# A decoder layer on one core: stacks by way of DRAM, output weights in the chunk stream, the last head by token halves, a third pair of heads

## The chip, the core and the metric

The kernel runs on one core of a Trainium2 chip. A core has five engines with instruction streams of their own: TensorE (PE, matmuls; PEld is its weight load), VectorE (DVE), ScalarE (ACT), GpSimd (POOL) and SyncE (SP), which here issues nearly all DMAs; 16 DMA engines move the data. The metric is the device time of one execution in microseconds, lower is better.

## What is computed

One layer of a decoder with two groups of four heads, 1024 tokens, model width 1024, all float32:

```python
u = rmsnorm(h, norm_pre_w)
dq, dk, dv, dg, rq, rk, rv, rg = split(u @ w_in)          # 8 x 512 columns
y_a = diff_attention(dq, dk, dv, positions, lam)          # p0 - lam * p1, causal softmax, rotary
y_a = rmsnorm(y_a, diff_subln_w) * (1 - lambda_init) * silu(dg)
y_b = rmsnorm(retention_chunkwise(rq, rk, rv, positions)) * silu(rg)
y = concat(y_a, y_b) @ w_out
out = h + rmsnorm(y, norm_post_w)
```

A differential head has two components (u = 0, 1) of 64 dimensions; each has its own scores and softmax, and the second probability matrix is subtracted, times lambda, from the first. Retention works in chunks of 128 tokens with a running state.

## The kernel before

Heads are numbered in the order of work, `HEADS = [0, 4, 1, 5, 2, 6, 3, 7]`: even places are differential heads, odd ones retention heads. Below, "head 6" is the head at place 6.

*Precision.* A float32 factor is split in a high and a low part (`whi`/`wlo` for weights, `uh`/`ul` for the input, `yh`/`yl` for the mixed heads), and every product is three matmuls: high x high, high x low, low x high.

*Main order.* `main_steps` walks through `ORDER`: projection blocks "qk" (queries and keys of one head; `cols_steps`, L404 to 421, lines L414 to L416, four groups g of 24 matmuls 512 wide, g // 2 is the half of the tokens, g % 2 the half of the rotation) and "vg" (values and gates; `rows_steps`, L386 to 402, lines L396 to L398, eight token tiles). A vg block of two heads has matmuls 512 wide, one of a single head 256 wide. In short: v01 q0 v23 q1 q2 v4 q3 q4 v5 q5 q6 v6 q7 v7, then the output projection `out_steps` (L766) for eight token tiles. v01 stands apart (`first_rows`, L377).

*Side streams.* `run` (L940) interleaves the main order with four streams: `score_stream` (scores and softmax of differential heads, `diff_scores` L531, two matmuls per component and piece of keys, L543), `value_stream` (transposes L599, values L612), `ret_stream` (L882; `ret_scores` L644 with transposes L650 and products L657, `ret_states` L669, `ret_out` L692/L693) and `last_stream` (L923; `prep_tile` L745 multiplies a tile of y by its gates, L749, transposes it, L758, and splits it). A step runs when a planner's clock has reached what it waits for; a main step is 1.36 us of matmuls. This order is worked out while the kernel is built and is then fixed: PE and SP run their instructions in exactly this order, so an instruction whose data is late holds up all behind it. The other engines' order is chosen by the scheduler.

*SP's queue.* All DMAs go through `dma` (L124): the planner books 0.6 us each. Moves and stores that are to be issued later wait in a list with a due time (`late`, L129), and `flush` (L134) issues those that are due as long as the booked queue is at most 1.0 us ahead of the clock.

*Weights.* `pump` (L225) fetches chunks of weights (128 x 512, 256 KB) four ahead into `raw`, and splits them (ACT copy L212, subtraction L190) into nine slots `whi`/`wlo`, which `drop_chunk` frees. A chunk is due 4.0 us after its fetch and 3.0 us after its split.

*Stacks.* A differential head's scores contract, in one matmul, the high and low parts: rows of the stack `ks` (128 partitions = hi 64, lo 64) and `qs` (128 partitions = the same 64 rows twice). `diff_qk` (L502) rotates a half of the tokens (`rotate`, L482, lines L490 to L499), splits it into `rhi` and `rlo` (L511, L190; one buffer each), and `move` (L514) copies it with 24 DMAs of 32 partitions (64 KB) from SBUF to SBUF: for each component u, part x and rotation half r one into `ks` and two into `qs`. They are due 4.0 us after the rotation's matmuls. When the last one of a component is issued, `ready` is set to its queue time + 3.6 us, and `score_stream` waits for it.

*Output weights.* `fetch_wout`, `split_wout` and `load_wout` (L709 to L734) read 16 tiles of `w_out` through the same `raw` buffers and split them on ACT (L727) and DVE (L728): columns 512 to 1023 (nh = 1) in places `block_steps` and `main_steps` name around v7, columns 0 to 511 (nh = 0) during v7, into the memory of `uh0`/`ul0`, which is read up to token tile 3 of the last block.

Of the kernel before, what the change touches and what calls it, by code (L numbers as in the profile page):

```python
# [10 lines left out]
F32 = mybir.dt.float32  # L11
F32R = mybir.dt.float32r
# [8 lines left out]
P = 128  # L21
# [4 lines left out]
H = 4  # L26
# [12 lines left out]

HEADS = [0, 4, 1, 5, 2, 6, 3, 7]
ORDER = [("vg", 0, 1), ("qk", 0), ("vg", 2, 3), ("qk", 1), ("qk", 2), ("vg", 4), ("qk", 3), ("qk", 4),
         ("vg", 5), ("qk", 5), ("qk", 6), ("vg", 6), ("qk", 7), ("vg", 7)]

CHUNKS = [(b, c) for b, blk in enumerate(ORDER) for c in range(8 if len(blk) == 3 else 4)]


def shape_constants():
# [38 lines left out]
def body(ctx, tc, x, xt_in, pos, wpk, wout, vecs, npre, npost, subln, cst, out):  # L88
# [101 lines left out]
        eng.tensor_tensor(dst, full, hi.bitcast(F32), op=ALU.subtract)  # L190

    raws, chunks, due_in, due_out = {}, {}, {}, {}
    ahead = {"fetched": 0, "split": 0, "held": 0}

    def fetch_chunk(pieces=1):

        b, c = CHUNKS[ahead["fetched"]]
        raw = raws[b, c] = wraw.tile([P, 512], F32, tag="raw", name="raw")
        for k in range(pieces):
            ks = slice(512 // pieces * k, 512 // pieces * (k + 1))  # L200
            dma(raw[:, ks], wpk[ahead["fetched"], :, ks])
        due_in[b, c] = queue[0] + 4.0
        ahead["fetched"] += 1

    def split_chunk(pieces=1):
        b, c = CHUNKS[ahead["split"]]
        raw = raws.pop((b, c))
        hi = whi.tile([P, 512], F32R, tag="whi", name="whi")
        lo = wlo.tile([P, 512], F32R, tag="wlo", name="wlo")
        for k in range(pieces):  # L210
            ks = slice(512 // pieces * k, 512 // pieces * (k + 1))
            nc.scalar.copy(hi[:, ks], raw[:, ks])  # L212
            split_lo(lo[:, ks], raw[:, ks], hi[:, ks])
        chunks[b, c] = (hi, lo)
        due_out[b, c] = clock[0] + 3.0
        ahead["split"] += 1
        ahead["held"] += 1

    def drop_chunk(b, c):

# [4 lines left out]
    def pump():  # L225

        while True:
            f, n = ahead["fetched"], ahead["split"]
            if f < len(CHUNKS) and (f < 4 or due_out.get(CHUNKS[f - 4], 1e9) <= clock[0]):
                fetch_chunk()  # L230
            elif n < f and ahead["held"] < NWB and due_in[CHUNKS[n]] <= clock[0]:
                split_chunk()
            else:
                return

    def ready(b, c):
        return lambda: due_out.get((b, c), 1e9) <= clock[0]

    def weight(b, kt):

# [261 lines left out]
    def diff_qk(st, g, ps):  # L502
        rotated = rotate(st, g, ps, (cosD, sinD))
        if rotated is None:
            return
        sl, o1, o2 = rotated
        need("m", 0)
        hi = dp["rot"].tile([P, 2, HT], F32R, tag="rhi", name="rhi")
        lo = dp["rot"].tile([P, 2, HT], F32R, tag="rlo", name="rlo")
        for r, o in enumerate((o1, o2)):  # L510
            nc.scalar.copy(hi[:, r, :], o)  # L511
            split_lo(lo[:, r, :], o, hi[:, r, :])

        def move(u, x, r):  # L514
            if (g, u, x, r) == (1, 0, 0, 0):

                st["q"] = dp["stk"].tile([P, 2, 2, S], F32R, tag="qs", name="qs")
                st["k"] = dp["stk"].tile([P, 2, S], F32R, tag="ks", name="ks")
            q0, k0, src = u * 32, 64 + u * 32, (hi, lo)[x]
            d = 64 * x + 32 * r  # L520
            mv(st["k"][d:d + 32, u, sl], src[k0:k0 + 32, r, :])
            for twice in range(2):
                d = 64 * twice + 32 * r
                mv(st["q"][d:d + 32, u, x, sl], src[q0:q0 + 32, r, :])
            if x and r:
                st["ready", g // 2, u] = queue[0] + 3.6

        for k in range(8):
            late(4.0, lambda k=k: move(k // 4, k // 2 % 2, k % 2), "m")

    def diff_scores(st, i, u):  # L531

# [171 lines left out]


    fp = {}
    wo = {"s": const.tile([P, 1], F32, name="wos")}

    def fetch_wout(nh, ms):  # L709
        for m in ms:  # L710
            raw = wraw.tile([P, 512], F32, tag="raw", name="raw")
            dma(raw, wout[HEADS[m] * P:(HEADS[m] + 1) * P, nh * 512:(nh + 1) * 512])
            wo[nh, m] = raw

    def split_wout(nh, ms):

        for m in ms:
            if nh == 0:
                if m == 0:
                    wo["h0"] = upool.tile([P, 8, 512], F32R, tag="uh0", name="woh0")  # L720
                    wo["l0"] = upool.tile([P, 8, 512], F32R, tag="ul0", name="wol0")
                wh, wl = wo["h0"][:, m, :], wo["l0"][:, m, :]
            else:
                wh = whi.tile([P, 512], F32R, tag="whi", name="woh")
                wl = wlo.tile([P, 512], F32R, tag="wlo", name="wol")
            raw, sc = wo[nh, m], wo["s"] if HEADS[m] < H else 0.5
            nc.scalar.activation(wh, raw, AF.Copy, scale=sc)  # L727
            nc.vector.scalar_tensor_tensor(wl, raw, sc, wh.bitcast(F32), op0=ALU.mult, op1=ALU.subtract)  # L728
            wo[nh, m] = (wh, wl)

    def load_wout(nh, ms):
        for m in ms:
            fetch_wout(nh, [m])
            split_wout(nh, [m])  # L734

    def load_y(t):
        yrows[t] = fp["y"].tile([P, D], F32, tag="yt", name="yt")
# [28 lines left out]
    def out_steps(t):  # L766
        rows = slice(t * P, (t + 1) * P)
        yh, yl = fp.pop(t)
        xt = fp["fp"].tile([P, D], F32, tag="xt2", name="xt2")
        dma(xt, x[rows, :])  # L770
        ob = fp["fp"].tile([P, D], F32, tag="ob", name="ob")
        sq = fp["fp"].tile([P, 512], BF16, tag="osq", name="osq")
        ms = sm_.tile([P, 2], F32, tag="ms2", name="ms2")
        for nh in range(2):
            op = bank("op")
            for m in range(8):
                wh, wl = wo[nh, m]
                nc.tensor.matmul(op, lhsT=yh[:, m, :], rhs=wh, start=(m == 0), stop=False)  # L778
                nc.tensor.matmul(op, lhsT=yh[:, m, :], rhs=wl, start=False, stop=False)  # L779
                nc.tensor.matmul(op, lhsT=yl[:, m, :], rhs=wh, start=False, stop=(m == 7))  # L780
                if m in (1, 3, 5):
                    yield 1.36
            sl = slice(nh * 512, (nh + 1) * 512)
            nc.scalar.activation(sq, op, AF.Square, scale=1.0 / math.sqrt(D), accum_out=ms[:, nh:nh + 1])
            if nh == 0:
                nc.vector.tensor_scalar(ms[:, 0:1], ms[:, 0:1], EPS, None, op0=ALU.add)
            else:
                tot = sm_.tile([P, 1], F32, tag="tot", name="tot")
                rsqrt(tot, ms[:, 1:2], ms[:, 0:1])
# [10 lines left out]

    heads = [{"n": n, "h": hh} for n, hh in enumerate(HEADS)]
    done = set()
    def block_steps(b):
        kind, sts = ORDER[b][0], [heads[n] for n in ORDER[b][1:]]
        n, st = ORDER[b][1], sts[0]
        if kind == "vg":
            for m in ORDER[b][1:]:

                yield lambda: m < 4 or ("A", m - 4) in done or ("R", m - 4) in done
            if len(sts) == 2:  # L810
                for t in range(NT):
                    ps = bank("pj")
                    yield from rows_steps(b, t, ps, 0, 1)
                    values_gates(sts, t, ps)
            else:
                for t in range(0, NT, 2):
                    ps = bank("pj")
                    for j in range(2):
                        yield from rows_steps(b, t + j, ps, j, 2)
                    values_gates(sts, t, ps)  # L820
                    if b == NB - 1 and t == 0:
                        fetch_wout(0, range(0, 4))
                    elif b == NB - 1 and t == 2:
                        split_wout(0, range(0, 4))
                        load_wout(0, range(4, 8))
                        fetch_wout(1, range(4, 8))
            return
        for g in range(4):
            if n > 1 and g == 1:

                yield lambda: ("S", n - 2) in done or ("R", n - 2) in done
            ps = yield from cols_steps(b, g)
            (diff_qk if st["h"] < H else ret_qk)(st, g, ps)
            if b == NB - 2 and g == 2:
                fetch_wout(1, range(0, 4))

    def main_steps():
        for b in range(1, NB):
            if b == NB - 1:
                split_wout(1, range(0, 4))  # L840
            yield from block_steps(b)
        split_wout(1, range(4, 8))
        for t in range(NT):
            yield lambda: fp.get(("ready", t), 1e9) <= clock[0]
            yield from out_steps(t)
# [257 lines left out]
```

## Time and profile before

| | us |
|---|---|
| median of three runs | 589.57 |
| lowest and highest run | 587.15, 591.94 |
| the profiled execution | 587.86 |
| its span, first to last instruction | 586.1 |
| PE busy in the span | 569.3 |

The profile belongs to one execution, whose span leaves 1.8 us around it. Matmuls overlap their neighbours, so the mean duration of one is longer than the distance between the starts of two; the distances are what the span is made of.

### The profile page before, as it was taken

Reading aid. Unit: us, or ns where it says so; the run is one execution under the profiler, and the core shown is the slowest. Engines: PE = TensorE matmul, PEld = TensorE weight load, DVE = VectorE, ACT = ScalarE, POOL = GpSimd, SP = SyncE. Lnnn points to the kernel's source line nnn. Section 1 sums busy time; section 2 is a strip of 40 time slices with the busy share of each in tenths; the row PEclk is TensorE's granted clock in tenths of the full one; section 3 lists DMA queues with packets and bytes.
Section 4 is the critical chain, followed back from the end, with each engine's and each line's share of the span. In section 5 each row is a group of like instructions: output and inputs, shape, how many; then the busy total and the mean of one; then the engine's idle time right before and its main releaser. Section 6 shows DMA issues by size and latency. Waiting matters only on the chain.

```text
span 586.1 us, 9508 instructions
## 1 busy us (share of the span) xinstructions
PE 569.3 (97%) x3280; PEld 499.7 (85%) x3280; DVE 321.7 (55%) x798; ACT 244.4 (42%) x682; POOL 133.7 (23%) x182
## 2 busy tenths in 40 slices
PE   6999999999999999999999999999999989999995
PEld 5888878788888999888899888899989978888884
DVE  4794426466355467744655755446775265544432
ACT  6696125457022366451346442336543362212120
POOL 4154221114124302233503032431222000000000
PEclk9999999999999999999999999999999989999999
DMA  8964764305242554112554124164123772455322
GB/s 276 340 242 122 182 163 130 87 20 156 61 107 50 134 129 140 46 55 77 140 132 117 49 47 125 47 158 96 54 54 93 245 242 101 168 181 195 108 73 107
DMA packets 49344, 73.98 MB, mean 126 GB/s; under 512 B 7824, under 2 KB 21520, under 8 KB 49296
## 3 DMA queue, kind: packets, MB, share of 16 engines
q1 hardware_dynamic: 49152, 73.36, 42.9%
q8 instruction: 26, 0.43, 0.3%
q14 instruction: 22, 0.18, 0.1%
q10 hardware_dynamic: 144, 0.00, 0.0%
HBM read 42.41 MB, written 12.06 MB: 93 GB/s over the span
## 4 chain that ended last, share of the span: by engine, by line
PE 93%; DMA 2%; SPq 1%; DVE 1%; issue 1%; ACT 1%; POOL 0%; DVEq 0%; POOLq 0%; ACTq 0%
PE pj L414 10%; PE pj L415 10%; PE pj L416 10%; PE pj L377 8%; PE pj L396 7%; PE pj L397 7%; PE pj L398 7%; PE sc L543 6%; PE o L612 5%; PE op L778 5%; PE op L780 5%; PE op L779 5%; PE tp L599 3%; SPq L127 1%; PE yt L758 1%; PE o L693 1%
## 5 line engine op out<-in xcount | busy, mean ns | idle before, releaser
L180 POOL TENSOR_TENSOR tot<-tot,halves 128x1 f32<-128x1 f32 (+1 forms) x56 | 33.4, 596 | 315.3 <-DVE tot L179 306.4
L414 PE MATMUL pj<-uh,whi 128*128 128x512 f32 x256 | 104.0, 406 | 0.0
L416 PE MATMUL pj<-uh,wlo 128*128 128x512 f32 x256 | 100.1, 391 | 0.0
L415 PE MATMUL pj<-ul,whi 128*128 128x512 f32 x256 | 99.9, 390 | 0.0
L396 PE MATMUL pj<-whi,uh 128*128 128x256 f32 (+1 forms) x320 | 99.5, 311 | 0.0
L398 PE MATMUL pj<-whi,ul 128*128 128x256 f32 (+1 forms) x320 | 97.4, 305 | 0.0
L397 PE MATMUL pj<-wlo,uh 128*128 128x256 f32 (+1 forms) x320 | 97.3, 304 | 0.0
L398 PEld LDWEIGHTS pj<-whi,ul 128*128 128x128 f32 x320 | 60.9, 190 | 2.6
L397 PEld LDWEIGHTS pj<-wlo,uh 128*128 128x128 f32 x320 | 61.0, 191 | 2.4
L396 PEld LDWEIGHTS pj<-whi,uh 128*128 128x128 f32 x320 | 60.9, 190 | 2.4
L416 PEld LDWEIGHTS pj<-uh,wlo 128*128 128x128 f32 x256 | 48.0, 188 | 10.5
L212 ACT CAST whi<-raw 128x512 fp32r<-128x512 f32 (+1 forms) x65 | 39.5, 619 | 41.5 <-PE pj L415 27.9
L414 PEld LDWEIGHTS pj<-uh,whi 128*128 128x128 f32 x256 | 48.2, 188 | 8.5
L415 PEld LDWEIGHTS pj<-ul,whi 128*128 128x128 f32 x256 | 48.3, 189 | 8.4
L778 PE MATMUL op<-woh,yh 128*128 128x512 f32 x128 | 51.4, 401 | 0.3 <-ACT yh L760 0.3
L780 PE MATMUL op<-woh,yl 128*128 128x512 f32 x128 | 50.2, 392 | 0.0
L779 PE MATMUL op<-wol,yh 128*128 128x512 f32 x128 | 50.1, 391 | 0.0
L190 POOL TENSOR_TENSOR wlo<-raw,whi 128x512 fp32r<-128x512 f32 x32 | 41.6, 1307 | 35.8 <-ACT whi L212 35.4
L543 PE MATMUL sc<-ks,qs 128*128 128x384 f32 (+5 forms) x192 | 42.9, 349 | 2.9 <-ACT v L452 1.3
L499 POOL TENSOR_TENSOR o<-o,m 128x512 f32<-128x512 f32 x16 | 27.1, 1694 | 58.9 <-DVE o L496 49.5
L612 PEld LDWEIGHTS o<-v,at 128*128 128x128 f32 x288 | 37.5, 191 | 2.4
L612 PE MATMUL o<-v,at 128*128 128x128 f32 x288 | 38.4, 274 | 0.0
(139 smaller groups left out, 976.5 us busy)
## 6 DMA issues: line engine op xcount, KB each, us to landing
raw<-in_wpk SPq DMA_DIRECT2D x63, 256.0 KB, 3.0
xr<-in_x SPq DMA_DIRECT2D x8, 512.0 KB, 8.7
gdram<-g SPq DMA_DIRECT2D x32, 128.0 KB, 2.1
qs<-rhi SPq DMA_DIRECT2D x64, 64.0 KB, 2.0
qs<-rlo SPq DMA_DIRECT2D x64, 64.0 KB, 2.0
raw<-in_wout SPq DMA_DIRECT2D x16, 256.0 KB, 4.4
gy<-gdram SPq DMA_DIRECT2D x8, 512.0 KB, 4.8
xt<-in_x SPq DMA_DIRECT2D x8, 512.0 KB, 4.0
```

The source lines that it names most:

```text
L377: nc.tensor.matmul(ps, rhs=wp, lhsT=up[half][:, kt, j * P:(j + 1) * P], start=(kt == 0 and n == 0), stop=(kt == KT - 1 and n == 2))
L396: nc.tensor.matmul(dst, lhsT=a, rhs=wh, start=(kt == 0 and j == 0), stop=False)
L397: nc.tensor.matmul(dst, lhsT=a, rhs=wl, start=False, stop=False)
L398: nc.tensor.matmul(dst, lhsT=l, rhs=wh, start=False, stop=(kt == KT - 1 and j == n - 1))
L414: nc.tensor.matmul(ps, lhsT=wh, rhs=uh[half][:, kt, :], start=(kt == 0), stop=False)
L415: nc.tensor.matmul(ps, lhsT=wh, rhs=ul[half][:, kt, :], start=False, stop=False)
L416: nc.tensor.matmul(ps, lhsT=wl, rhs=uh[half][:, kt, :], start=False, stop=(kt == KT - 1))
L543: nc.tensor.matmul(sp[:, 0:kn], lhsT=st["q"][:, u, x, i * P:(i + 1) * P], rhs=st["k"][:, u, k0:k0 + kn], start=(x == 0), stop=(x == 1))
L612: nc.tensor.matmul(o_ps[:, 0:P], lhsT=at[:, j * P:(j + 1) * P], rhs=v[:, j0 + j, :], start=(j0 + j == 0), stop=(j0 + j == i))
L778: nc.tensor.matmul(op, lhsT=yh[:, m, :], rhs=wh, start=(m == 0), stop=False)
L779: nc.tensor.matmul(op, lhsT=yh[:, m, :], rhs=wl, start=False, stop=False)
L780: nc.tensor.matmul(op, lhsT=yl[:, m, :], rhs=wh, start=False, stop=(m == 7))
```

## The change

*Stacks.* `move` gives way to `store` and `load`. For each half of the tokens, four stores of 256 KB (part x, rotation half r; all 128 partitions of `rhi` or `rlo`) go into a DRAM tile `sd`, due 3.0 (x = 0) and 3.7 us (x = 1) after the matmuls; six loads of 256 KB, due at 7.0 us, fill the stacks: per component one for `ks` (hi and lo) and two for `qs` (a broadcast of two copies each). `ready` is set as before, at queue time + 3.6 us. SP waits for the stores before it issues the loads that read them.

*Output weights.* The 16 tiles are appended to the chunks (`STREAM`); `pump` fetches and splits them like chunks, nh = 0 once `ahead["u0"]` is set (after v7a), nh = 1 into free `whi`/`wlo` slots. `out_steps` waits, for tile 0, for each chunk by the planner's clock.

*Halves.* Blocks v6, q7 and v7 are cut into token halves a and b: v01 q0 v23 q1 q2 v45 q3 q4 q5 v6a q6 v6b q7a v7a q7b v7b.

*Third pair.* v4 and v5 become v45, 512 wide, between q2 and q3.

```diff
-ORDER = [("vg", 0, 1), ("qk", 0), ("vg", 2, 3), ("qk", 1), ("qk", 2), ("vg", 4), ("qk", 3), ("qk", 4),
-         ("vg", 5), ("qk", 5), ("qk", 6), ("vg", 6), ("qk", 7), ("vg", 7)]
+PLAN = "v01 q0 v23 q1 q2 v45 q3 q4 q5 v6a q6 v6b q7a v7a q7b v7b".split()
+BLOCKS = list(dict.fromkeys(w.rstrip("ab") for w in PLAN))
+ORDER = [("vg" if w[0] == "v" else "qk",) + tuple(int(c) for c in w[1:]) for w in BLOCKS]
...
+STREAM = CHUNKS + [("out", nh, m) for nh in range(2) for m in range(8)]
...
+            if key[0] == "out":
+                _, nh, m = key
+                dma(raw, wout[HEADS[m] * P:(HEADS[m] + 1) * P, nh * 512:(nh + 1) * 512])
...
+    def room(key):
+
+        return ahead["u0"] if key[:2] == ("out", 0) else ahead["held"] < NWB
...
+        if key[0] == "out":
+
+            sc = wo["s"] if HEADS[key[2]] < H else 0.5
+            nc.scalar.activation(hi, raw, AF.Copy, scale=sc)
+            nc.vector.scalar_tensor_tensor(lo, raw, sc, hi.bitcast(F32), op0=ALU.mult, op1=ALU.subtract)
...
-            if f < len(CHUNKS) and (f < 4 or due_out.get(CHUNKS[f - 4], 1e9) <= clock[0]):
+            if f < len(STREAM) and (f < 4 or due_out.get(STREAM[f - 4], 1e9) <= clock[0]):
                 fetch_chunk()
-            elif n < f and ahead["held"] < NWB and due_in[CHUNKS[n]] <= clock[0]:
+            elif n < f and room(STREAM[n]) and due_in[STREAM[n]] <= clock[0]:
                 split_chunk()
...
-        def move(u, x, r):
-            if (g, u, x, r) == (1, 0, 0, 0):
-
+        sd = dram.tile([2, 4, 2, 32, HT], F32, tag="sd", bufs=2, name="sd")
+
+        def store(x, r):
+            dma(sd[x, :, r], (hi, lo)[x][:, r, :].bitcast(F32))
+
+        def load(u, part):
+            if (g, u, part) == (1, 0, 0):
                 st["q"] = dp["stk"].tile([P, 2, 2, S], F32R, tag="qs", name="qs")
                 st["k"] = dp["stk"].tile([P, 2, S], F32R, tag="ks", name="ks")
-            q0, k0, src = u * 32, 64 + u * 32, (hi, lo)[x]
-            d = 64 * x + 32 * r
-            mv(st["k"][d:d + 32, u, sl], src[k0:k0 + 32, r, :])
-            for twice in range(2):
-                d = 64 * twice + 32 * r
-                mv(st["q"][d:d + 32, u, x, sl], src[q0:q0 + 32, r, :])
-            if x and r:
+            if part == 0:
+                dma(st["k"][:, u, sl].bitcast(F32), sd[:, 2 + u].rearrange("x r p c -> x (r p) c"))
+                return
+            x = part - 1
+            src = sd[x, u].rearrange("r p c -> (r p) c").unsqueeze(0).broadcast_to([2, 64, HT])
+            dma(st["q"][:, u, x, sl].bitcast(F32), src)
+            if x:
                 st["ready", g // 2, u] = queue[0] + 3.6
 
-        for k in range(8):
-            late(4.0, lambda k=k: move(k // 4, k // 2 % 2, k % 2), "m")
+        for x in range(2):
+            for r in range(2):
+                late(3.0 + 0.7 * x, lambda x=x, r=r: store(x, r), "m")
+        for u in range(2):
+            for part in range(3):
+                late(7.0, lambda u=u, part=part: load(u, part), "m")
...
+                if t == 0:
+                    yield ready("out", nh, m)
+                wh, wl = chunks["out", nh, m]
...
+        tokens = (0, NT) if half is None else (half * NT // 2, (half + 1) * NT // 2)
...
-        for g in range(4):
+        for g in range(tokens[0] // 2, tokens[1] // 2):
...
+        last = max(k for k, w in enumerate(PLAN) if w[-1] == "a")
+        for k, w in enumerate(PLAN[1:], 1):
+            yield from block_steps(BLOCKS.index(w.rstrip("ab")), "ab".index(w[-1]) if w[-1] in "ab" else None)
+            ahead["u0"] = k >= last
```

## Rows read from the trace of the kernel before

**Rows 1.** The page's part 1: busy us, share of the span and instructions of each engine.
```profile
PE 569.3 (97%) x3280; PEld 499.7 (85%) x3280; DVE 321.7 (55%) x798; ACT 244.4 (42%) x682; POOL 133.7 (23%) x182
```

**Rows 2.** Waits of PE: line, releaser, us in total, times, longest.
```profile
PE pj L377 <- ACT whi L212: 5.1, 1, 5.1
PE yt L758 <- DVE yt L749: 2.2, 1, 2.2
PE sc L543 <- ACT v L452: 1.3, 1, 1.3
PE sc L543 <- DMA qs<-rlo: 1.1, 1, 1.1
PE sc L543 <- issue: 0.5, 1, 0.5
PE op L778 <- ACT yh L760: 0.3, 1, 0.3
```

**Rows 3.** Timeline of head 7's start and the final projection: start, us, engine, line, operation.
```profile
460.33 0.38 PE L650 MATMUL tp<-ident,kT 128*128 128x128 f32 x2
...
475.06 0.60 PE L758 MATMUL yt<-ident,yt 128*128 128x128 f32 x4
...
476.41 0.74 DVE L728 SCALAR_TENSOR_TENSOR wol<-raw,wos,woh 128x512 fp32r<-128x512 f32 x1
...
477.06 0.68 DVE L749 TENSOR_TENSOR yt<-yt,gy 128x512 f32<-128x512 f32 x1
...
477.89 0.73 PE L758 MATMUL yt<-ident,yt 128*128 128x128 f32 x4 [2.23 <-DVE yt L749]
```

**Rows 4.** Busy us by engine, granted clock, DMA share, GB/s of 475 to 482 us.
```profile
475.00:482.00 7.00, 4.42 (x21) 3.43 (x21) 6.09 (x11) 4.94 (x12) 0.77 (x2) 0.76 0.82 258
```

**Rows 5.** PE's timeline: first and next instruction of two undisturbed stretches, and q2's end.
```profile
263.01 0.39 PE L414 MATMUL pj<-uh,whi 128*128 128x512 f32 x1
...
275.26 0.38 PE L650 MATMUL tp<-ident,kT 128*128 128x128 f32 x2
...
463.72 0.28 PE L397 MATMUL pj<-wlo,uh 128*128 128x256 f32 x1
...
467.91 0.27 PE L693 MATMUL o<-v,sT 128*128 128x128 f32 x1
...
188.82 0.39 PE L693 MATMUL o<-v,sT 128*128 128x128 f32 x2
...
194.50 0.28 PE L396 MATMUL pj<-whi,uh 128*128 128x256 f32 x1
```

**Rows 6.** Timelines of DVE, POOL, SP and PE: head 6's first stacks and its scores.
```profile
371.90 0.69 DVE L495 TENSOR_TENSOR m<-pj,sinD 128x512 f32<-128x512 f32 x1 [0.72 <-PE pj L416]
...
374.46 0.55 SPq L127 DMA_DIRECT2D ks<-rhi  x1
...
376.97 1.29 POOL L190 TENSOR_TENSOR rlo<-o,rhi 128x512 fp32r<-128x512 f32 x1
...
381.02 1.22 SPq L127 DMA_DIRECT2D qs<-rlo  x2
...
386.82 0.34 PE L543 MATMUL sc<-ks,qs 128*128 128x128 f32 x2
...
394.96 1.56 PE L543 MATMUL sc<-ks,qs 128*128 128x128 f32 x10
```

**Rows 7.** DMA issues: tensors, queue, count, KB each, median us from issue to landing.
```profile
raw<-in_wpk SPq DMA_DIRECT2D x63, 256.0 KB, 3.0
...
gdram<-g SPq DMA_DIRECT2D x32, 128.0 KB, 2.1
...
xk<-in_xt SPq DMA_DIRECT2D x8, 256.0 KB, 4.6
```

**Rows 8.** As rows 4, of the first 30 us and of 560 to 580 us.
```profile
0.00:30.00 30.00, 24.86 (x98) 20.35 (x99) 19.23 (x31) 19.76 (x31) 7.58 (x16) 1.00 0.92 310
...
560.00:580.00 20.00, 19.93 (x88) 16.15 (x87) 5.18 (x11) 2.07 (x6) 0.55 (x1) 1.00 0.29 106
```

More of the change, by code (lines that the diff above doesn't have):

```diff
@@ L192, in body @@
     raws, chunks, due_in, due_out = {}, {}, {}, {}
-    ahead = {"fetched": 0, "split": 0, "held": 0}
+    wo = {"s": const.tile([P, 1], F32, name="wos")}
+    ahead = {"fetched": 0, "split": 0, "held": 0, "u0": False}
     def fetch_chunk(pieces=1):
-        b, c = CHUNKS[ahead["fetched"]]
-        raw = raws[b, c] = wraw.tile([P, 512], F32, tag="raw", name="raw")
+        key = STREAM[ahead["fetched"]]
+        raw = raws[key] = wraw.tile([P, 512], F32, tag="raw", name="raw")
         for k in range(pieces):
             ks = slice(512 // pieces * k, 512 // pieces * (k + 1))
-            dma(raw[:, ks], wpk[ahead["fetched"], :, ks])
-        due_in[b, c] = queue[0] + 4.0
+            if key[0] == "out":
+                _, nh, m = key
+                dma(raw, wout[HEADS[m] * P:(HEADS[m] + 1) * P, nh * 512:(nh + 1) * 512])
+            else:
+                dma(raw[:, ks], wpk[ahead["fetched"], :, ks])
+        due_in[key] = queue[0] + 4.0
         ahead["fetched"] += 1
+    def room(key):
+        return ahead["u0"] if key[:2] == ("out", 0) else ahead["held"] < NWB
     def split_chunk(pieces=1):
[L206 to L210, printed above, removed]
+        key = STREAM[ahead["split"]]
+        raw = raws.pop(key)
+        if key[:2] == ("out", 0):
+            if key[2] == 0:
+                wo["h0"] = upool.tile([P, 8, 512], F32R, tag="uh0", name="woh0")
+                wo["l0"] = upool.tile([P, 8, 512], F32R, tag="ul0", name="wol0")
+            hi, lo = wo["h0"][:, key[2], :], wo["l0"][:, key[2], :]
+        else:
+            hi = whi.tile([P, 512], F32R, tag="whi", name="whi")
+            lo = wlo.tile([P, 512], F32R, tag="wlo", name="wlo")
+            ahead["held"] += 1
+        if key[0] == "out":
+            sc = wo["s"] if HEADS[key[2]] < H else 0.5
+            nc.scalar.activation(hi, raw, AF.Copy, scale=sc)
+            nc.vector.scalar_tensor_tensor(lo, raw, sc, hi.bitcast(F32), op0=ALU.mult, op1=ALU.subtract)
+        for k in range(0 if key[0] == "out" else pieces):
             ks = slice(512 // pieces * k, 512 // pieces * (k + 1))
@@ L213, in split_chunk @@
             split_lo(lo[:, ks], raw[:, ks], hi[:, ks])
-        chunks[b, c] = (hi, lo)
-        due_out[b, c] = clock[0] + 3.0
+        chunks[key] = (hi, lo)
+        due_out[key] = clock[0] + 3.0
         ahead["split"] += 1
-        ahead["held"] += 1
     def drop_chunk(b, c):
@@ L234, in pump, with ready @@
                 return
-    def ready(b, c):
-        return lambda: due_out.get((b, c), 1e9) <= clock[0]
+    def ready(*key):
+        return lambda: due_out.get(key, 1e9) <= clock[0]
     def weight(b, kt):
@@ L706, in body @@
     fp = {}
[L707 to L734, printed above, removed]
     def load_y(t):
@@ L776, in out_steps @@
             for m in range(8):
-                wh, wl = wo[nh, m]
+                if t == 0:
+                    yield ready("out", nh, m)
+                wh, wl = chunks["out", nh, m]
                 nc.tensor.matmul(op, lhsT=yh[:, m, :], rhs=wh, start=(m == 0), stop=False)
@@ L802, in body, with block_steps @@
     done = set()
-    def block_steps(b):
+    def block_steps(b, half=None):
         kind, sts = ORDER[b][0], [heads[n] for n in ORDER[b][1:]]
         n, st = ORDER[b][1], sts[0]
+        tokens = (0, NT) if half is None else (half * NT // 2, (half + 1) * NT // 2)
         if kind == "vg":
@@ L810, in block_steps @@
             if len(sts) == 2:
-                for t in range(NT):
+                for t in range(*tokens):
                     ps = bank("pj")
@@ L815, in block_steps @@
             else:
-                for t in range(0, NT, 2):
+                for t in range(*tokens, 2):
                     ps = bank("pj")
@@ L820, in block_steps @@
                     values_gates(sts, t, ps)
[L821 to L826, printed above, removed]
             return
-        for g in range(4):
+        for g in range(tokens[0] // 2, tokens[1] // 2):
             if n > 1 and g == 1:
@@ L833, in block_steps @@
             (diff_qk if st["h"] < H else ret_qk)(st, g, ps)
-            if b == NB - 2 and g == 2:
-                fetch_wout(1, range(0, 4))
     def main_steps():
[L838 to L842, printed above, removed]
+        last = max(k for k, w in enumerate(PLAN) if w[-1] == "a")
+        for k, w in enumerate(PLAN[1:], 1):
+            yield from block_steps(BLOCKS.index(w.rstrip("ab")), "ab".index(w[-1]) if w[-1] in "ab" else None)
+            ahead["u0"] = k >= last
         for t in range(NT):
```

## The prediction

> **What bounds the kernel now.** I read the page's busy times first, then the waits of TensorE (PE), then its timeline. PE is busy for 569.3 of 586.1 us, VectorE for 55%, ScalarE and GpSimd for less, and the weight loads run beside the matmuls [rows 1]: time goes only if PE gets less work or waits less. All its waits are six, 10.5 us together [rows 2]; the first (5.1 us, first weights) is not touched. Two places are within the change's reach. Early, the first head's scores wait 1.1 us for a stack, 0.5 us more without a shown cause (I read it as the other component's stack) and 1.3 us for a drained bank. Late, at 475 us, the final projection is late. There the second half of the first y tile is transposed 2.23 us late, because VectorE had splits of output weights (L728, the last one 0.74 us at 476.41) ahead of the product (L749) [rows 3]. From 475 to 482 us the granted clock is 0.76 [rows 4], that is, 24% of 7 us = 1.7 us lost at the lower of its two levels. With the waits of 2.2 and 0.3 us [rows 2] this place costs 4.2 us. After PE's last matmul comes a tail of some 6 us, unchanged.
>
> **The change, part by part.**
>
> *Third pair 512 wide.* Matmuls of 512 columns start 54 in 12.25 us, 0.2269 us each; those of 256 columns 35 in 4.19 us, 0.1197 us each [rows 5]. Blocks v4 and v5 have 2 x 192 narrow ones; v45 has 192 wide ones: 192 x (2 x 0.1197 - 0.2269) = 2.4 us less. The pair also waits for retention head 1, which now ends some 5 us before v45 begins (its last matmuls start at 188.8 us, v4 at 194.5 us [rows 5]): nothing lost.
>
> *Output weights in the stream, last head by halves.* Same 16 fetches, ScalarE and VectorE splits, but one at a time, four raw tiles ahead, from the end of v7a on. Behind v7a stand q7b (48 x 0.2269 = 10.9 us) and v7b (96 x 0.1197 = 11.5 us), 22.4 us. Head 7's retention needs 14.7 us from its first transposes (460.33 us) to the first y tile (475.06 us) [rows 3], and the plan adds 0.9 + 2.5 us until the output matmuls: 18.1 us, under 22.4 us if head 6's attention ends with v7a. A round of four chunks takes 0.6 + 4.0 + 3.0 us by the plan, so eight chunks are there some 11 us after v7a and all sixteen at 26 us, when the second half of columns is wanted at 28 us. The 4.2 us go; I keep 0.5 us for a split that still stands ahead of L749: -3.7 us. Should the attention end 5 us later than v7a, 1 to 2 us come back.
>
> *Stacks by way of DRAM, work on the queue.* SP issues 24 transfers a half and head today, ten after: 192 become 80, at 0.6 us some 67 us of SP. SP is not PE, so this is no term by itself. It is what now places the scores: in head 6 the second product of q6 is out at 371.9 us (zero below), component 0's last move goes at 381.6, the first score runs at 386.8 and component 1's at 395.0 (+14.9, +23.1) [rows 6]. With ten transfers the plan's due times (stores 3.0 and 3.7, loads 7.0, 0.6 each, two a step of 1.36 us, then 3.6) put them at +13.2 and +15.2. The second half follows 10.9 us later, at +24 and +26, and block 4's scores, which the plan's softmax costs hold back 13.4 us, at +27 and +30.
>
> *Stacks, the wait added.* A load waits on SP until the stores have landed. Behind it on SP stand weight fetches, y and gate stores, and in the end PE, whose order is fixed. The stores need rlo, whose second half is done at 378.3 us, +6.4 [rows 6]. The transfers are 256 KB each. No row shows this store or this load. Nearest by size are the weight chunk (256 KB from DRAM, 3.0 us), the gate store (128 KB to DRAM, 2.1 us) and, from above, 256 KB of x at 4.6 us [rows 7]. With 2.6 us for a store and 3.0 us for a load: stores landed at +9.0, three loads issued by +10.8 and landed near +13.8, against +13.2 planned. That is 0.5 us late a head, 2 us for four, against 1.6 us of today's stack waits; the bank wait I keep. Then this part costs 0.4 us, and with 0.5 us for PE's new neighbours the sum is -2.4 - 3.7 + 0.4 + 0.5 = -5.2 us.
>
> *Stacks, how a transfer is spread.* Those prices hold if all 16 DMA engines share a load. In the kernel before, every transfer counts 128, 64 or 32 rows outermost, so all can be dealt to 16 without remainder, and in none do the landings tell who carried it. The new ones count otherwise: both kinds of load name two halves outermost (the key load its hi and lo, the query load a broadcast of two copies), the store four groups of 32 rows. If the outermost count is what is dealt out, two engines carry a load and four a store. The rate of one busy engine is read from two stretches: 310 GB/s at a share of 0.92 of 16 is 21.1 GB/s, 106 GB/s at 0.29 is 22.8 [rows 8]; with few in flight I take 22.8. A load is then 131,072 B / 22.8 = 5.75 us of its engines against 0.7 us, a store 2.9 us, and I take them to lie on the same engines, so that they add: 4 x 2.9 + 6 x 5.75 = 46 us a half and head. Of the chunk's 3.0 us, 2.3 us are not data; I put 0.8 us ahead of it and 1.5 us behind. The first store goes at +3.0, the stores' data end at +15.3 and have landed at +16.8; the loads' data start at +17.6, component 0 has landed at +36.4, component 1 at +53.6. The second half's stores queue behind them, landed at +65.1; its loads at +84.7 and +101.9. Planned were +13, +15, +24 and, by the scores that ask last, +30. PE, in order, stands four times a head, in all 101.9 - 30 = 71.9 us.
>
> The ends are thus 0.5 us and 71.9 us a head. I take the upper one. The chunk is nearest in bytes, but every row has an outermost count that 16 divides, so none bears on the point that decides, and I see nothing in the rows by which two would become sixteen.
> The Trainium skill speaks on this in "DMA: Bandwidth & Descriptors", section "Rules for kernel authors": a leading zero-stride broadcast of c copies keeps the whole transfer on at most c engines; its section on why a DMA increments its semaphore by 16 takes the largest count up to 16 that divides the outermost count of both sides. By it a load has two engines and a store four; no run here shows it yet.
>
> **The sum.** The profiled execution took 587.9 us (span 586.1 and 1.8 around it); the median of the runs shown is 589.6, 1.7 more. 587.9 - 5.2 = 582.7; + 4 x 71.9 = 870.3; + 1.7 = 872.0. **I forecast 872 us.** Not in it: the clock, which falls in waits like these (1.7 us a time [rows 4], 16 waits, up to 27 us), and weight fetches held up behind SP and behind the loads (up to some 8 us a head).
>
> **Rivals.** *Spread over 16 engines.* A load lands in about 3 us, the stacks are on time, and the gains stand: 582.7 + 1.7 = 584.4 us, not slower than before. For it: every 256 KB transfer of the trace so far behaves so. Against: none of them has this shape. It decides as long as a load lands within some 4 us; it gives 580 us if every wait in the change's reach goes (-2.4 - 4.2 - 2.9 from the median), 588 us if the gain at the final projection is missed.
> *Spread, but the round trip is late.* If stores and loads land like x (4.6 us), each head's first score is (4.6 - 2.6) + (4.6 - 3.0) = 3.6 us later: 14.4 us, 584.4 + 14.4 = 598.8 us. For it: head 0's score already waits for a stack [rows 2]. Against: the x transfers are issued back to back in the first 20 us, at a DMA share of 0.92 [rows 8].
> *Narrow, but the halves don't add.* If stores and loads lie on different engines, only the first half's lateness is left: 53.6 - 15.2 less 2 us of work, some 36 us a head: 584.4 + 144 = 728 us. Against: nothing in the rows puts them apart, and one engine in common is enough to add them.
>
> **Chances.** Narrow spread 0.70 (the third rival 0.05 of it), spread over 16 in time 0.22, spread but late 0.08. A measurement of this kernel tells about 1% from no change (the three runs span 0.8%). Spread in time splits evenly around -1% (583.7 us): faster 0.11, same 0.11. The late case lies at +1.5%, mostly slower: same 0.12 in all, slower 0.77. The narrow case's own range is 730 to 960: below, one half's cost only; above, the 21.1 GB/s rate (+23 us), the clock (+27) and fetches (+32). The whole range goes down to 580, into the in-time case, so that little more than one in ten is left out.
>
> **What would show it.** Right: the landing of the new loads near 7 us for the first of a group and tens of us for the last; sixteen long waits of PE's scores for their stacks, a PE share near 65%, a DMA share that rises while GB/s per busy engine stays; long SP waits of the loads for the stores; PE's clock low after the waits. Right for the rest: no PE wait at the final projection, 64 wide matmuls more per line of the row blocks and 128 narrow ones fewer. Wrong: loads landing in 3 us with PE over 96% busy; then the forecast falls as a whole, to 584.4 us.

## The result and the profile after

The changed kernel takes 871.4 us (870.9 to 871.5) against 588.9 us (587.2 to 591.9): a ratio of 1.479, 95% interval 1.472 to 1.485. The forecast was 872 us. The profiled execution took 871.5 us, with a span of 869.8 us.

First the page of the changed kernel: busy times, the clock row, and the packets.

```profile
span 869.8 us, 8933 instructions
PE 609.2 (70%) x3088; PEld 518.9 (60%) x3088; DVE 320.7 (37%) x798; ACT 244.2 (28%) x674; POOL 132.9 (15%) x182
...
PEclk9999568599997586799995576999658589999999
...
DMA packets 49565, 82.31 MB, mean 95 GB/s; under 512 B 4976, under 2 KB 17648, under 8 KB 49520
```

Against [rows 1], PE has 3088 matmuls in place of 3280: the 192 wide ones of the third pair replace 384 narrow ones. Its idle time went from 16.8 us (586.1 - 569.3) to 260.6 us (869.8 - 609.2), so +243.8; its busy time rose by 39.9 us, though the wide pair takes 2.4 us of work away by the prediction's sum. Together that is the 283.7 us of the span. The clock row shows why the busy time rose: in eleven of the 40 slices the granted clock is at 5 or 6 tenths, near the lower of its two levels (1.2 of 2.4 GHz).

PE's waits in the changed kernel (in all, times, longest; us):

```profile
PE sc L577 <- DMA qs<-sd: 245.5, 32, 21.7
PE pj L401 <- ACT whi L237: 5.5, 1, 5.5
PE rs L703 <- ACT kr L686: 2.5, 1, 2.5
...
```

One line holds it all: PE's scores wait for stacks loaded from DRAM, 32 times, 61 us a head. The waits of [rows 2] look small beside it. What the stacks wait for is in the transfers. The DMA view of head 0's loads, 100 to 110 us, cut into 40 slices (busy share of 16 DMA engines in tenths, then GB/s):

```profile
DMA  1111111111111111111111111111111111111111
GB/s 49 49 49 49 49 49 49 49 49 49 49 49 49 49 49 49 49 49 49 49 49 49 49 49 49 49 49 49 49 49 49 49 49 49 49 49 49 49 49 49
```

And the same stretch as one window (length, then busy time of PE, PE loads, DVE, ACT, POOL, granted clock, DMA share, GB/s):

```profile
100.00:110.00 10.00, 3.44 (x9) 2.71 (x10) 0.52 (x3) 0.46 (x2) 0.00 (x0) 0.50 0.13 49
```

A share of 0.13 fits two busy engines of 16 (0.125), at a level rate of 49 GB/s: 24.5 GB/s each; the packets below settle the count. So a load of 262,144 B takes 5.35 us. SP's timeline of head 0's second half (start, duration; us) shows the same pace from the issuing side:

```profile
120.85 3.93 SPq L131 DMA_DIRECT2D sd<-rlo  x2
135.46 0.55 SPq L131 DMA_DIRECT2D ks<-sd  x1
136.06 3.70 SPq L131 DMA_DIRECT2D qs<-sd  x2
139.80 5.10 SPq L131 DMA_DIRECT2D ks<-sd  x1
144.94 10.49 SPq L131 DMA_DIRECT2D qs<-sd  x2
155.47 6.44 SPq L131 DMA_DIRECT2D gdram<-g  x2
```

Of the time from 124.78 to 135.46 us, SP spends 10.5 us in waits for the stores' landing. The first load then goes in 0.55 us, the next two take 3.70 us together; from the fourth on an issue takes 5.1 to 5.2 us, about the time of one load on two engines. Whatever stands behind them on SP, gate stores here, waits as long.

**The landings, against the forecast's.** Head 4 (block q4): the second product on VectorE, which the forecast takes as zero, then PE's first scores on each stack, with the idle time before them.

```profile
440.43 0.68 DVE L519 TENSOR_TENSOR m<-pj,sinD 128x512 f32<-128x512 f32 x1
```

```profile
471.00 0.45 PE L577 MATMUL sc<-ks,qs 128*128 128x128 f32 x1 [16.56 <-DMA qs<-sd]
476.26 0.47 PE L577 MATMUL sc<-ks,qs 128*128 128x128 f32 x1 [4.81 <-DMA qs<-sd]
...
493.17 2.71 PE L577 MATMUL sc<-ks,qs 128*128 128x128 f32 x9 [5.32 <-DMA qs<-sd]
...
525.01 1.17 PE L577 MATMUL sc<-ks,qs 128*128 128x320 f32 x3 [4.65 <-DMA qs<-sd]
...
541.73 2.45 PE L577 MATMUL sc<-ks,qs 128*128 128x320 f32 x7 [4.87 <-DMA qs<-sd]
```

A component waits twice, for its first and for its second query part; the rows left out are the first of the other three. The stacks are complete at 476.26, 493.17, 525.01 and 541.73 us, that is +35.8, +52.7, +84.6 and +101.3. Forecast were +36.4, +53.6, +84.7 and +101.9. Counted the same way, heads 2 and 6 lie within 1.9 us of the forecast; head 0 is 3.5 to 6.0 us later than it, as SP issues its first store 8.3 us after the product, not 3.0.

So the halves do add, and the third rival (728 us) is out. Whether they add by the engines that they share or by SP, which issues this head's second stores only at 487.31 us, behind the first half's loads, no run separates.

### The profile page after: what moved, and what is told of

The parts are those of the page before. It is cut to its first block, busy times and chain, and to the rows that moved or that the text cites. A ratio compares the mean times of both kernels' runs of the same rounds, so it can differ in the third digit from the quotient of the medians.

```text
span 869.8 us, 8933 instructions
## 1 busy us (share of the span) xinstructions
PE 609.2 (70%) x3088; PEld 518.9 (60%) x3088; DVE 320.7 (37%) x798; ACT 244.2 (28%) x674; POOL 132.9 (15%) x182
## 2 busy tenths in 40 slices
DMA packets 49565, 82.31 MB, mean 95 GB/s; under 512 B 4976, under 2 KB 17648, under 8 KB 49520
## 3 DMA queue, kind: packets, MB, share of 16 engines
q1 hardware_dynamic: 49376, 81.74, 29.6%
## 5 line engine op out<-in xcount | busy, mean ns | idle before, releaser
L577 PE MATMUL sc<-ks,qs 128*128 128x384 f32 (+5 forms) x192 | 60.0, 437 | 245.5 <-DMA qs<-sd 245.5
L577 PEld LDWEIGHTS sc<-ks,qs 128*128 128x128 f32 x192 | 40.9, 246 | 258.0 <-issue 152.0
L420 PE MATMUL pj<-whi,uh 128*128 128x512 f32 (+1 forms) x256 | 94.9, 371 | 0.0
L421 PE MATMUL pj<-wlo,uh 128*128 128x512 f32 (+1 forms) x256 | 91.8, 359 | 0.0
L422 PE MATMUL pj<-whi,ul 128*128 128x512 f32 (+1 forms) x256 | 91.7, 358 | 0.0
L581 DVE CUSTOM_DVE_ANT_0 sc<-sc,mask 128x128 f32<-128x128 f32 (+3 forms) x32 | 15.8, 499 | 141.2 <-PE sc L577 140.8
L586 DVE TENSOR_REDUCE nm<-sc 128x1 f32<-128x320 f32 (+3 forms) x32 | 18.8, 589 | 120.1 <-PE sc L577 120.1
L602 ACT ACTIVATE p<-sc,nm 128x384 f32<-128x384 f32 (+5 forms) x48 | 27.6, 579 | 126.2 <-DVE nm L581 124.2
L422 PEld LDWEIGHTS pj<-whi,ul 128*128 128x128 f32 x256 | 52.7, 206 | 6.2
L602 ACT ACTIVATE sc<-sc,nm 128x384 f32<-128x384 f32 (+5 forms) x48 | 26.4, 551 | 105.9 <-DVE nm L581 88.7
```

The lines of the kernel that those rows point to most:

```text
L420: nc.tensor.matmul(dst, lhsT=a, rhs=wh, start=(kt == 0 and j == 0), stop=False)
L421: nc.tensor.matmul(dst, lhsT=a, rhs=wl, start=False, stop=False)
L422: nc.tensor.matmul(dst, lhsT=l, rhs=wh, start=False, stop=(kt == KT - 1 and j == n - 1))
L577: nc.tensor.matmul(sp[:, 0:kn], lhsT=st["q"][:, u, x, i * P:(i + 1) * P], rhs=st["k"][:, u, k0:k0 + kn], start=(x == 0), stop=(x == 1))
L602: nc.scalar.activation(probs[b], sps[b][:, 0:kn], AF.Exp, scale=-1.0 if b == np_ - 1 else 1.0, bias=nm[:, np_ - 1:np_], accum_out=ss[:, b: ...
```

## The experiments

### How many engines carry a transfer

The first three kernels leave the transfers, their bytes, their order and their due times alone and change only which dimension stands outermost. *Loads wide:*

```diff
-dma(st["k"]..., sd[:, 2 + u].rearrange("x r p c -> x (r p) c"))
+dma(st["k"]..., sd[:, 2 + u].rearrange("x r p c -> (r p) x c"))
-src = sd[x, u].rearrange("r p c -> (r p) c").unsqueeze(0).broadcast_to([2, 64, HT])
+src = sd[x, u].rearrange("r p c -> (r p) c").unsqueeze(1).broadcast_to([64, 2, HT])
```

*Stores wide* (the scratch tensor holds rows as p r, so a store names 128 rows; loads still two halves outermost):

```diff
-sd = dram.tile([2, 4, 2, 32, HT], ...)
+sd = dram.tile([2, 4, 32, 2, HT], ...)
-dma(sd[x, :, r], ...)
+dma(sd[x, :, :, r].rearrange("g p c -> (g p) c"), ...)
```

*Both wide* has both edits.

> The changed kernel with one difference: the loads name the 64 rows outermost and the two halves inside them (the stack's rows are paired row by row), the same bytes in the same six loads. Theory (the outermost count sets how many DMA engines carry a transfer): the loads go from two engines to sixteen, some 0.7 us of data each, only the stores stay on four (2.9 us each, landed at +16.8), so each head's first score is some 7 us late and nothing after it: 612 to 625 us. Rival (the trip through DRAM itself, or SP waiting for the stores, is what costs): above 800 us.

> The changed kernel with one difference: the stores name 128 rows outermost (another layout of the DRAM tile), the loads keep their two halves outermost. Theory: the stores land some 9 us earlier in each of the eight halves, the loads still take 5.2 us each on two engines: 871 - 70 = about 800 us, with the long waits for qs<-sd still there. Rival (the stores' landing is the main cost): under 650 us. Rival (the trip itself): 871 us.

> Both differences together: all ten transfers of a half with 64 or 128 rows outermost, same bytes, same number, same order on every engine. Theory: what the prediction had for sixteen engines, 584 us by the old median (580 to 590), ratio to before 0.985 to 1.0. Rival (round trip late, 4.6 us a landing): 599 us, ratio 1.017. Rival (the trip itself costs): above 800 us.

Measured: 658.7 us with the loads wide and 803.5 us with the stores wide (one run each), 595.4 us (591.1 to 596.9) with both; the ratio of the last to the kernel before is 1.010, interval 1.006 to 1.013. The line of PE's waits for stacks, of each in this order:

```profile
PE sc L577 <- DMA qs<-sd: 56.0, 16, 13.6
```

```profile
PE sc L577 <- DMA qs<-sd: 181.0, 32, 12.8
```

```profile
PE sc L577 <- DMA qs<-sd: 8.1, 6, 3.3
```

276.0 of the 282.5 us are back when nothing but the order of the dimensions changes, so the spread is the cause. The loads alone are worth 212.7 us, the stores alone 67.9 us. Each edit takes off its own share, together 280.6 us. Loads wide came out above the 612 to 625 us expected. The four stores of a half still take some 10.7 us of their four engines (an estimate: 4 x 262,144 B at the loads' 24.5 GB/s an engine), which the expectation had; but PE waits 56.0 us, 14 us a head where I expected 7, and is busy for 586.3 us, 17.0 us more than before, for which I had nothing.

The packets give a second reading that needs no time. Their rows with loads wide, stores wide, both wide:

```profile
DMA packets 50237, 82.31 MB, mean 125 GB/s; under 512 B 5648, under 2 KB 18320, under 8 KB 50192
```

```profile
DMA packets 49949, 82.31 MB, mean 103 GB/s; under 512 B 5360, under 2 KB 18032, under 8 KB 49904
```

```profile
DMA packets 50621, 82.32 MB, mean 138 GB/s; under 512 B 6032, under 2 KB 18704, under 8 KB 50576
```

Suppose that a transfer leaves one small packet on each engine that it uses. The kernel before has 457 transfers in its trace and 7824 packets under 512 B on its page; with 16 engines each, 457 x 16 = 7312 of them, 512 are left for others. The changed kernel has 457 - 192 + 80 = 345 transfers: 265 on 16 engines, 48 loads on 2, 32 stores on 4 make 4240 + 96 + 128 = 4464, and with the 512 others 4976, the number on its page. With the loads on 16 the same sum is 5648, with the stores on 16 it is 5360, with both 6032. All agree to the packet.

### The rest of the change without the round trip

The changed kernel with the 24 moves of before in place of the store and load (pair, stream and halves stay):

```diff
-        for x in range(2): ... late(3.0 + 0.7 * x, lambda x=x, r=r: store(x, r), "m")
-        for u in range(2): ... late(7.0, lambda u=u, part=part: load(u, part), "m")
+        for k in range(8):
+            late(4.0, lambda k=k: move(k // 4, k // 2 % 2, k % 2), "m")
```

> The changed kernel with the stacks filled by the 24 moves of before: the other three edits alone. Theory: 2.4 us from the wide pair and 3.7 us from the final projection, 6 us under before, ratio 0.990 (0.984 to 0.995), no long PE wait left but the first head's. Rival (one of the three edits also costs): ratio above 1.0.

Measured: 590.6 us (589.6 to 592.9), ratio 1.0025, interval 1.0003 to 1.0046. The gain that I had summed for these parts, 2.4 + 3.7 us, is not there. PE's waits, after the one for the first weights:

```profile
PE op L778 <- ACT yh L758: 2.1, 1, 2.1
...
PE yt L756 <- DVE yt L747: 1.1, 3, 0.6
PE tp L625 <- DVE p L609: 1.0, 2, 0.7
PE tp L625 <- ACT p L594: 0.6, 1, 0.6
```

The wait of the y tiles for VectorE is down from 2.2 to 1.1 us as foreseen, but the first output product now waits 2.1 us for ScalarE's copy of the y tile, and the stretch still has a low clock (0.86 from 475 to 487 us, a loss of 1.7 us):

```profile
475.00:487.00 12.00, 9.06 (x43) 7.11 (x42) 8.15 (x16) 4.76 (x11) 0.00 (x0) 0.86 0.81 280
```

The waits of transposes for probabilities (1.0 + 0.6 us) are new, too. What stands ahead of the copy is in the timeline (start, duration, idle time before), and the DMA engines are full meanwhile (470 to 482 us, share 1.04):

```profile
478.27 0.72 ACT L233 ACTIVATE whi<-raw,wos 128x512 fp32r<-128x512 f32 x1 [6.43 <-DMA raw<-in_wout]
...
480.04 0.58 ACT L758 CAST yh<-yt 128x512 fp32r<-128x512 f32 x1
...
480.67 0.50 PE L778 MATMUL op<-woh,yh 128*128 128x512 f32 x1 [2.07 <-ACT yh L758]
```

```profile
470.00:482.00 12.00, 9.06 (x67) 7.95 (x66) 5.38 (x12) 5.07 (x16) 0.90 (x2) 0.99 1.04 342
```

ScalarE stands 6.43 us before a split whose output weight has not landed; the copy of the y tile is behind it, and PE waits 2.07 us for that copy. Both-wide shows the same with another copy behind the split, that of the keys:

```profile
482.71 0.72 ACT L233 ACTIVATE whi<-raw,wos 128x512 fp32r<-128x512 f32 x1 [1.99 <-DMA raw<-in_wout]
...
485.24 0.78 PE L703 MATMUL rs<-v,kr 128*128 128x128 f32 x4 [2.02 <-ACT kr L686]
```

That late weights cost the gain was tried with one constant, in the kernel with the old moves:

```diff
-        due_in[key] = queue[0] + 4.0
+        due_in[key] = queue[0] + (8.0 if key[0] == "out" else 4.0)
```

> The version with the old moves, the pair, the stream and the halves (590.6 us), with one constant changed: a fetched output weight is due for its split 8.0 us after its issue, not 4.0. Theory: near the end the DMA engines are full, so output weights land later than planned, and the split that waits for one on ScalarE holds up the copies of keys and y tiles behind it, for which PE waits; with splits placed after the landing the gain of the final projection that I predicted comes back in part: 587 to 589 us, a ratio to before of 0.995 to 0.999, and ScalarE no longer waits for an output weight. Rival: the waits at the end come from gates and y rows that land late on the same full engines, or the output products then wait for their weights; 590 to 592 us.

Measured: 589.2 us (586.5 to 590.3), ratio 1.0008, interval 0.9988 to 1.0028. PE's wait for the y tile's copy is gone and the clock of that stretch (475 to 487 us) is full, but the y tiles' wait for VectorE is 3.2 us again:

```profile
PE yt L756 <- DVE yt L747: 3.2, 3, 2.3
```

The two intervals overlap, so the 1.4 us between the medians is not a measured gain. ScalarE does still wait for output weights, 5.3 us in four waits (6.8 us in two before), so that part of the expectation misses. PE's first wait goes as the theory has it; that the next thing late at that place takes what it leaves fits the rows, but no run shows it by itself.

### The pair alone

The kernel before, with heads 4 and 5 in one block:

```diff
-... ("qk", 2), ("vg", 4), ("qk", 3), ("qk", 4), ("vg", 5), ("qk", 5), ...
+... ("qk", 2), ("vg", 4, 5), ("qk", 3), ("qk", 4), ("qk", 5), ...
```

> The kernel before with one edit: heads 4 and 5 share a value and gate block 512 wide; the moves, the output weights and the last head are as before. Theory (the prediction's first term): 192 wide matmuls in place of 384 narrow ones, 2.4 us of PE less, so a ratio of 0.996 and PE busy at 566.9 us, with the waits of before left as they were. Rival: the side work that filled the two narrow blocks now meets other neighbours and a wait of 1 to 3 us comes in, ratio 0.999 to 1.002.

Measured: 596.9 us (595.5 to 599.8), ratio 1.015, interval 1.012 to 1.019: worse than either theory. The row blocks did become as counted (128 wide and 128 narrow matmuls on each of their three lines, against 64 and 256), but beside [rows 2] a wait of PE's projections for VectorE's probabilities is new (3.4 us), the one of the output products for the y tile has gone from 0.3 to 2.6 us, and the y tiles' from 2.2 to 2.6 us.

```profile
PE pj L414 <- DVE p L583: 3.4, 1, 3.4
PE yt L758 <- DVE yt L749: 2.6, 2, 2.4
PE op L778 <- ACT yh L760: 2.6, 1, 2.6
```

The first falls in a stretch that was smooth before. From 350 to 375 us, first with the pair alone, then before:

```profile
350.00:375.00 25.00, 21.52 (x134) 18.55 (x133) 16.63 (x58) 13.82 (x49) 4.83 (x12) 0.93 0.10 28
```

```profile
350.00:375.00 25.00, 25.00 (x154) 22.01 (x153) 12.71 (x30) 7.20 (x24) 7.55 (x11) 1.00 0.32 81
```

ScalarE has 13.8 us of work there, not 7.2: as I read it, the block that leaves takes away the projections between which one head's softmax was spread, and PE meets VectorE and ScalarE in a bunch. No run tests this, and why the plan bunches it there was not followed up.

### When the plan takes a stack for ready

Both wide, and the scores placed later:

```diff
-                st["ready", g // 2, u] = queue[0] + 3.6
+                st["ready", g // 2, u] = queue[0] + 7.5
```

> The version with both kinds of transfer wide (595.4 us), with one constant changed: the plan takes a stack to be ready 7.5 us after its last load is issued, not 3.6. Theory: the 8.1 us of stack waits and the low clock behind them (7.75 us of excess at 75 to 100 us in all) come only from scores placed too early for a round trip of this length; PE does block work there instead, so 587 to 590 us, a ratio to before of 0.997 to 1.002, with no wait for a stack above 0.5 us. Rival: later scores are late for what follows them (value products, the last head's retention, the output), and the time moves to other waits: 593 to 597 us.

Measured: 584.8 us (582.6 to 585.9), ratio 0.993, interval 0.991 to 0.996; better than expected. From 78 to 92 us the version with 3.6 had a clock of 0.76 and 5.4 us without a matmul; with 7.5 the whole stretch has its full clock:

```profile
78.00:92.00 14.00, 8.56 (x33) 6.80 (x32) 4.82 (x15) 3.89 (x11) 3.13 (x3) 0.76 0.82 279
```

```profile
75.00:100.00 25.00, 23.45 (x110) 19.25 (x109) 12.68 (x41) 10.20 (x33) 4.79 (x4) 1.00 0.78 258
```

Its waits for stacks are 1.5 us in all, two of them, so "none above 0.5 us" was too much to expect.

To see whether it is the constant alone, the same 7.5 with the old moves:

> The version with the old moves, the pair, the stream and the halves (590.6 us), with the stack's ready constant at 7.5 us in place of 3.6. It tells whether the gain of the version with wide transfers and this constant (584.8 us) is that of the constant or of the way by DRAM. Theory: the old moves' 1.8 us of stack waits go and little else, since they landed near the plan: 588 to 590 us, so the way by DRAM is worth the rest, some 4 us. Rival: the later scores are what helps, with either transfer: 584 to 586 us.

Measured: 604.2 us (602.1 to 606.9), ratio 1.023, interval 1.019 to 1.027. Both expectations miss: later scores make the old moves slower by 13.6 us. Its waits lie in other places:

```profile
PE sc L569 <- ACT v L476: 4.8, 1, 4.8
PE tp L625 <- DVE p L609: 4.6, 1, 4.6
...
```

So a later score is no gain by itself: the same constant gains 10.6 us where the stacks land later than planned (both wide) and costs 13.6 us where they had kept PE waiting for 1.8 us only. Why the old moves lose so much by it was not followed up.

Both constants with both transfers wide:

> Both retimings together: wide stores and loads, a stack ready 7.5 us after its last load is issued, an output weight due for its split 8.0 us after its fetch. Theory: the two act in different stretches (75 to 100 us and 460 to 485 us), so this one has the gain of the first (584.8 us) and some 1 us of what is still lost at the end there (3.2 us of excess at 450 to 475 us): 583 to 584.5 us, a ratio to before of 0.990 to 0.993. Rival: at the end the splits only trade places with what waits there, and the time is that of the version with the first retiming alone, 584 to 586 us.

Measured: 582.1 us (580.7 to 586.4), ratio 0.987, interval 0.983 to 0.991. This is the best version found, 1.3% under the kernel before and a little below both expectations. Its interval touches that of the version with the first constant alone (0.991 to 0.996), so what the second constant adds is not settled.

### Narrow transfers with a plan that knows of them

The changed kernel, all transfers narrow, and one constant:

```diff
-                st["ready", g // 2, u] = queue[0] + 3.6
+                st["ready", g // 2, u] = queue[0] + 45.0
```

> The changed kernel with its narrow stores and loads, and one constant changed: the plan takes a stack to be ready 45 us after its last load is issued, not 3.6, so that PE is given other work meanwhile. Theory: the price is that of landings that come later than the order of PE assumes; a half head costs some 42 us of its two and four DMA engines (4 stores at 102 GB/s, 6 loads at 49 GB/s), eight halves 336 us, and that has room beside 580 us of PE, so much of the loss goes: 640 to 720 us, with stack waits well under half of 245.5 us. Rival: SP, which blocks while its loads find no room, holds up the weight fetches, and PE then waits for weights or for the next head instead: over 760 us.

Measured: 852.8 us (one run), 18.6 us less than the changed kernel. The time is the rival's. PE no longer waits for stacks at all; its longest waits are now

```profile
PE sc L577 <- ACT v L476: 74.7, 4, 45.6
PE tp L684 <- DMA kT<-o: 71.8, 1, 71.8
PE pj L438 <- ACT whi L237: 54.3, 1, 54.3
...
```

The 54.3 us can be followed back. SP, then VectorE, ScalarE and PE:

```profile
144.65 10.49 SPq L131 DMA_DIRECT2D qs<-sd  x2
155.19 18.65 SPq L131 DMA_DIRECT2D gdram<-g  x6
```

```profile
170.12 0.42 DVE L473 SCALAR_TENSOR_TENSOR g<-th,pj 128x256 f32<-128x256 f32 x1 [76.38 <-DMA gdram<-g]
```

```profile
170.57 0.37 ACT L476 ACTIVATE v<-pj,rs 128x128 f32<-128x128 f32 x1 [72.55 <-DVE g L473]
```

```profile
175.08 0.79 PE L438 MATMUL pj<-uh,whi 128*128 128x512 f32 x1 [54.28 <-ACT whi L237]
```

The loads hold SP until 155.14 us; the gate stores behind them go only then, VectorE has no free gate tile until one has landed, ScalarE stands behind VectorE with a weight split behind that, and PE waits for the split. So it is gate stores, more than the weight fetches that the rival names, by which SP holds PE up here. The other two long waits stand behind the same thing: gate stores (before the 45.6 us wait ends) and a retention head's keys (the 71.8 us wait) are issued at 324.66 and 496.65 us, right behind a head's last loads. A transfer on two engines thus costs not only its own landing: it holds the queue from which everything else is issued. Whether another engine's queue would free SP was not tried.

## Why the prediction was right, point by point

**The spread (+71.9 us a head): right, and shown.** Two engines a load and four a store, by the packets, by the flat 49 GB/s, and by the edits that change the order of dimensions alone. This agrees with the Trainium skill, "DMA: Bandwidth & Descriptors", section "Rules for kernel authors": a leading broadcast of two copies keeps a transfer on at most two engines. The key load, which broadcasts nothing, went the same way by its two outermost halves, and turning the copies to an inner place was enough to undo it.

**The sizes in it: two errors that cancel, which is luck.** A load takes 5.35 us of its engines, not 5.75 (24.5 GB/s an engine, not 22.8), and weight fetches run among the loads on the same two engines. Within head 4 a component's three loads come 16.9 us apart (476.26 to 493.17), 5.6 us each, so the landings of that head agree within 1 us.

**The waits and the clock.** I summed 71.9 us of idle time a head and put up to 27 us of low clock outside the sum. Measured are 61.4 us idle a head (245.5 / 4) and 39.9 us more of PE's busy time in all, 10.0 a head: 71.4 together. As I read it, the low clock is no term of its own, since a load's landing sets when the next scores run, and PE's slower work between two landings only takes from the wait. From 440 to 542 us, the stretch of head 4, the clock is 0.67, and PE's 41.73 us of work do fit between the landings:

```profile
440.00:542.00 102.00, 41.73 (x167) 33.30 (x166) 23.89 (x68) 13.78 (x43) 13.41 (x15) 0.67 0.23 72
```

My "sixteen long waits" are 32: a component waits for both query parts. That moves nothing, as the last landing counts. Two other signs miss: PE's share is 70%, not near 65%, and the share of the DMA engines' time did not rise but fell, from 42.9% to 29.6% on the main queue, since the span grew and their work did not (some 251 and 257 us of 16 engines).

**Weight fetches (up to 8 us a head, outside the sum): not there.** In the changed kernel PE waits for no weight but the first. Where PE no longer asks for stacks so early, in the run with 45 us, it does wait for split weights (54.3 + 15.0 us), the longer one by way of the gate stores.

**The final projection (-3.7 us): this step failed.** I argued that the 4.2 us "go" because the weights' splits have time. With the old moves the place still loses 2.1 + 1.1 us in waits and 1.7 us to the clock. The splits now stand ahead of ScalarE's copies, and their weights land late on full DMA engines (6.43 us of idle ScalarE), which I had not priced. In the changed kernel itself a wait of 2.5 us for the keys' copy stands at that place.

**The wide pair (-2.4 us): the count right, the term not shown as time.** The pair alone is 1.5% slower. "Nothing lost" was reasoned from the retention head that the pair waits for, not from the softmax work; that this lost its cover is a reading, not shown.

**The round trip, if wide (+0.4 us): too small.** With both wide the query loads of head 0 land in 4.8 us and its lo stores in 6.0 us (medians; at a DMA share of 0.82 from 78 to 92 us), not in 3.0 and 2.6, and PE loses 8.1 us to stacks. The DMA view of that version, 75 to 105 us (count, KB each, median us to landing):

```profile
qs<-sd SPq DMA_DIRECT2D x8, 256.0 KB, 4.8
...
sd<-rlo SPq DMA_DIRECT2D x3, 256.0 KB, 6.0
```

Spread, the kernel would have come out near my second rival (598.8 forecast, 595.4 measured), not the first (584.4), but only in part by that rival's mechanism: against the old moves the round trip costs 4.8 us (595.4 - 590.6), not the 14.8 us that the rival's sum has; the rest is the gain that the other parts didn't bring.

So the sign and most of the size rest on one step, which was right. That the total is only 0.6 us off is luck. By the edits the narrow stacks cost 276.0 us against wide ones and 280.8 us against the old moves (871.4 - 590.6), 69.0 or 70.2 a head, not 71.9: 7 to 12 us less in all than I summed. The small terms beside it (-5.2 us in all) were wrong by some 6 to 11 us the other way (590.6 and 595.4 us in the two versions without narrow transfers, against 584.4).

## What to carry to other kernels

Before counting transfers, read each transfer's outermost dimension: a copy or a half put there can cut the engines that carry it to two, and moving it inward took no byte and no transfer more here. A slow transfer is paid for on its queue as well as where it lands: a plan that merely waits longer for it won back 18.6 of 282.5 us. And a plan with fixed due times must be given the landing that the profile shows: with the right layout, two such constants turned 1% slower into 1.3% faster, while a moved block and a later score without cause left it 1.5% and 2.3% slower than before.

## What was not expected of the hardware

An issue on SP, 0.55 us for the first load of the group shown, takes 5.1 to 5.2 us from the fourth on, about the pace at which two DMA engines carry one load away (5.35 us); the profile doesn't say on what the issue waits. And the count of packets under 512 B tells how many engines the transfers used: 4976, 5360, 5648 and 6032 in four kernels that differ in nothing but the order of the dimensions.
